# An expert layer on one core: two loads of x with other rows, and two copies behind each group of transposes

## The chip, the cores and the metric

The kernel runs on one core of a Trainium2 chip. Its engines work side by side and wait for each other through semaphores: TensorE (PE; PEld are its weight loads), VectorE (DVE), ScalarE (ACT), GpSimd (POOL) and SyncE (SP). Sixteen DMA engines move data between the memory of the chip (HBM, "dram" in the profile) and the core's own SBUF; transfers are issued here from SP's queue and from POOL's, and POOL's also turn float32 into bfloat16 on the way. TensorE writes into PSUM, from where DVE and ACT copy to SBUF. SBUF and PSUM have 128 partitions.

The metric is the device time of one execution in microseconds. Before the change it is 179.24 us, the median of three runs (179.19 to 179.28).

## The reference

Eight experts, each with its own 256 tokens of 512 numbers, go through two matrices with a ReLU between them:

```python
n_experts, capacity, hidden, expert_hidden = 8, 256, 512, 2048
# x  [8, 256, 512]   w1 [8, 512, 2048]   w2 [8, 2048, 512], all float32

def reference(x, w1, w2):
    h = np.matmul(x, w1)
    h = np.maximum(h, 0)
    return np.matmul(h, w2).astype(np.float32)
```

x is 4.2 MB, each of w1 and w2 is 33.6 MB, the output 4.2 MB.

## The kernel before

All matrix work is in bfloat16. The 2048 rows of x (experts one after the other, 512 numbers of 2 KB each) are laid over the partitions 16 at a time: partition p holds rows 16p to 16p+15, which are 32 KB of memory in one run (R is 16). The first six of them (HEAD) come through SP: a float32 load into a part of `out_sb` that is still free (L136, the first instruction of SP), which DVE then casts into `x_sb` (L215). The other ten come through POOL, which casts in the transfer (L154). `x_sb` is no buffer of its own; it lies in slot 2 of `w2_sb`.

TensorE needs x with the hidden dimension on the partitions, so it transposes it first (loop `transposes`). One turn of the loop takes every fourth column (turn ko, K1 = 4 turns). In a turn there are two groups of eight 128x128 transposes, one into each of two PSUM buffers `xt_ps[m]`; group m takes the rows r with r = 2·r2 + m of every partition, r2 = 0 to 7. Behind group 0 DVE copies `xt_ps[0]` to `xT`, behind group 1 ACT copies `xt_ps[1]` (both `copy_xt`, L206 to L210). The copy also puts the columns in order: PSUM has them by r2 and then by partition, `xT` by partition and then by r2, so that each expert's tokens lie together. TensorE takes `c_xt[0]` or `c_xt[1]` before it writes a buffer again, and both once more behind the loop (L331). Before the loop it waits for DVE's cast, for the identity matrix and for POOL's half of x (L324 to L326).

Then a loop over the experts. An expert takes `c_w1`, makes its hidden layer in four groups of 16 matmuls (`half`, twice), each of which ACT turns into `hT` with a ReLU (L240), takes `c_w2` and adds up two output tiles in 32 matmuls, which DVE copies to `out_sb` (L226; the very last one ACT, L246).

The weights come through POOL alone, in the order of the list `loads`: w1 and w2 for experts 0 and 1 together, the same for 2 and 3, w1 for 4 and 5, then w2 of 4, w2 of 5, and w1 and w2 of 6 and of 7, the last w2 in two halves. There are four slots for each matrix. Three kinds of wait stand in POOL's program in front of its transfers: w2 of experts 2 and 3 waits for all transposes, because its slot holds x (L172); each load into a used slot waits until the expert that used it is through; the stores wait for the outputs. SP waits for each load in turn (L143) and then tells TensorE through `c_w1` and `c_w2`. At the end SP stores the last expert's output (L146), POOL all the others (L194).

Lines to know: L136 and L154 load x; L172 is POOL's wait for the transposes; L191 issues the weights; L207 is the copy out of PSUM; L276 stands for every matmul and transpose, since all go through one helper.

Of the kernel before, what the change touches and what calls it, by code (L numbers as in the profile page):

```python
# [16 lines left out]
def kernel(  # L17
# [7 lines left out]
    nc = tc.nc  # L25
    P = 128
    E, C, H = x.shape
    F = w1.shape[2]
    MC = C // P
# [3 lines left out]
    R = E * C // P  # L33

    HEAD = 6
# [10 lines left out]

    x_v = x.rearrange("e (pp r) k -> (e pp) (r k)", r=R)
    w1_v = w1.rearrange("e (p ko) n -> p e (ko n)", ko=K1)  # L50
    w2_v = w2.rearrange("e (p h j) n -> p e h (j n)", h=2, j=JH)
    out_v = out.rearrange("e (p mo) k -> p e (mo k)", mo=MC)
# [4 lines left out]
    def allot(name, shape, dtype):  # L57
        nonlocal free
        places[name] = free
        t = nc.alloc_sbuf_tensor_at(name, shape, dtype, offset=free)  # L60
        free += math.prod(shape[1:]) * mybir.dt.size(dtype)
        return t
# [5 lines left out]
    xT = allot("xT", [P, K1, MC, E * P], BF16)  # L68
# [4 lines left out]
    x_sb = w2_sb[:, 2, :]  # L73
    X_AT = W2_AT + 2 * K2 * H * 2

    xt_ps = [nc.alloc_psum_tensor(f"xt_ps{i}", [P, R // MC, P], BF16) for i in range(MC)]
# [5 lines left out]
    def sem(name):  # L82
        s = nc.alloc_semaphore(name)
        sems.append(s)
        return s

    d_last, d_pool = sem("d_last"), sem("d_pool")
# [6 lines left out]
    d_head, d_half = sem("d_head"), sem("d_half")  # L94
# [38 lines left out]

    x_head = out_sb[:, :HEAD // MC].rearrange("p e m h -> p (e m h)")

    head = nc.sync.dma_start(x_head, x_v[:, :HEAD * H]).then_inc(d_head, 16)  # L136
    tc.info.no_tile_sem_insts.add(head.ins.name)
    tc.close()
    tc.compile()  # L139
# [11 lines left out]


    pool = nc.gpsimd
    pool.dma_start(x_sb[:, HEAD * H:], x_v[:, HEAD * H:]).then_inc(d_pool, 16)  # L154
    pool.memset(identity[:], 0.0).then_inc(s_event)  # L155
    pool.wait_ge(s_event, 1)

# [9 lines left out]
    for i, (w, es, h, n) in enumerate(loads):  # L167
# [17 lines left out]
        e, ne, at_slot = es[0], len(es), es[0] % NS  # L185
# [18 lines left out]


    def copy_xt(copy, ko, m):  # L206
        return copy(  # L207
            xT[:, ko, m].rearrange("k (ep r2) -> k ep r2", r2=R // MC),
            xt_ps[m][:].rearrange("k r2 ep -> k ep r2"),
        )  # L210


    dve = nc.vector
# [3 lines left out]
    for ko in range(K1):  # L217
        dve.wait_ge(*after_transposes(ko * MC + 1))
        copy_xt(dve.tensor_copy, ko, 0).then_inc(c_xt[0])
# [14 lines left out]
    for ko in range(K1):  # L234
        act.wait_ge(*after_transposes(ko * MC + 2))
        copy_xt(act.copy, ko, 1).then_inc(c_xt[1])
# [239 lines left out]
```

## Time and profile before

| | |
|---|---|
| median of three runs | 179.24 us |
| the profiled execution | 179.49 us, of which its span is 178.2 us |
| TensorE busy | 127.1 us (71% of the span) |
| DVE / ACT / POOL busy | 16.4 / 38.7 / 10.2 us |
| DMA: POOL's queue / SP's queue | 38.54 MB / 2.10 MB |
| read from HBM / written to it | 71.30 MB / 4.20 MB |
| mean granted TensorE clock | 0.943 |

The span runs from the first to the last instruction; the time of an execution has some more around it. A digit in a line of slices is the busy share of one fortieth of the span in tenths. A row of a group of instructions has the line, the engine, the operation, what it writes and reads, how often, then busy time and the mean of one in ns, then the idle time of the engine ahead of them and what ended it. A row in order of time begins with its start and its length in us. The sizes and rates of a transfer count what is written; where POOL's transfer casts, twice as much is read.

### The profile page before, as it was taken

To read this page: it belongs to the slowest core of one execution; us is meant where nothing else is said; L and a number is where in the kernel's file an instruction comes from. 1 tells how busy PE (TensorE), PEld (TensorE's weight loads), DVE (VectorE), ACT (ScalarE), POOL (GpSimd) and SP (SyncE) were. 2 spreads that over 40 slices of the span, in tenths; PEclk is the share of its full clock that TensorE was granted. 3 is DMA by queue.
4 is the path that set the end of the run, shared out by engine and by line. 5 is a ranking of instruction groups with operands and counts; after the bars stand their busy time and mean duration, and the time that the engine had idled before them with its cause. 6 is when DMAs were issued, how large, how long until landed. Compare 5 with 4: busy or idle time off the path is not lost. (4 is left out here: it accounts for less than half of the span.)

```text
span 178.2 us, 2076 instructions
## 1 busy us (share of the span) xinstructions
PE 127.1 (71%) x832; PEld 89.6 (50%) x832; DVE 16.4 (9%) x20; ACT 38.7 (22%) x38; POOL 10.2 (6%) x21
## 2 busy tenths in 40 slices
PE   0007620692039999994069999999999999949991
PEld 0006520592013695594024884794695695438740
DVE  0303420000000200110000200200200200020001
ACT  2002420053000053044000251152062044004401
POOL 4300010000000002001000100100010000001000
PEclk9999999999657999999759999999999999978999
DMA  5999999999999999998998999999999999999998
GB/s 199 299 212 232 232 195 221 232 195 221 232 210 206 232 217 199 232 224 191 232 228 188 235 228 195 224 232 195 221 232 195 221 232 210 206 204 223 298 418 328
DMA packets 3744, 40.63 MB, mean 228 GB/s; under 512 B 288, under 2 KB 288, under 8 KB 1312
## 3 DMA queue, kind: packets, MB, share of 16 engines
q0 software_dynamic: 3456, 38.54, 96.9%
q1 hardware_dynamic: 288, 2.10, 3.1%
HBM read 71.30 MB, written 4.20 MB: 424 GB/s over the span
## 5 line engine op out<-in xcount | busy, mean ns | idle before, releaser
L276 PE MATMUL o_ps<-w_sb,hT 128*128 x256 | 59.8, 394 | 19.5 <-PEq L99 19.5
L276 PE MATMUL h_ps<-xT,w_sb 128*128 x512 | 61.2, 282 | 11.8 <-PEq L99 11.8
L276 PEld LDWEIGHTS h_ps<-xT,w_sb 128*128 x512 | 57.8, 146 | 16.1 <-issue 12.5
L240 ACT ACTIVATE hT<-h_ps 128x1024 bf16<-128x1024 f32 x32 | 32.7, 1023 | 111.2 <-PE h_ps L276 111.2
L276 PEld LDWEIGHTS o_ps<-w_sb,hT 128*128 128x128 bf16 x256 | 25.3, 101 | 51.5 <-issue 24.5
L226 DVE COPY out_sb<-o_ps 128x512 f32<-128x512 f32 x15 | 9.7, 686 | 141.3 <-PE o_ps L276 141.3
L276 PE MATMUL xt_ps<-identity,w_sb 128*128 128x128 bf16 x64 | 7.6, 313 | 16.0 <-PEq L99 16.0
L276 PEld LDWEIGHTS xt_ps<-identity,w_sb 128*128 x64 | 6.5, 148 | 16.7 <-issue 16.7
L191 POOL DMA_DIRECT2D w_sb<-in_w_dram x12 | 7.4, 618 | 103.4 <-PE h_ps L276 57.1
L207 ACT COPY xT<-xt_ps 128x1024 bf16<-128x1024 bf16 x4 | 4.0, 1012 | 17.3 <-PE xt_ps L276 17.3
L207 DVE COPY xT<-xt_ps 128x1024 bf16<-128x1024 bf16 x4 | 4.9, 1224 | 10.1 <-PE xt_ps L276 10.1
L194 POOL DMA_DIRECT2D out_dram<-out_sb x1 | 1.0, 964 | 34.2 <-DMA out_dram<-out_sb 34.2
L215 DVE CAST w_sb<-out_sb 128x3072 bf16<-128x3072 f32 x1 | 1.8, 1760 | 7.2 <-DMA out_sb<-in_x_dram 7.2
L246 ACT COPY out_sb<-o_ps 128x512 f32<-128x512 f32 x1 | 0.6, 585 | 5.9 <-PE o_ps L276 5.9
L207 ACT ACT_TABLE_LOAD x1 | 1.3, 1283 | 2.0 <-PEq L139 2.0
L182 POOL DMA_DIRECT2D out_dram<-out_sb x1 | 0.5, 509 | 14.7 <-DVEq L229 14.7
L154 POOL DMA_DIRECT2D w_sb<-in_x_dram x1 | 0.7, 682 | 2.0 <-POOLq L139 2.0
L158 POOL TENSOR_SCALAR_AFFINE_SELECT identity<-identity 128x128 bf16<-128x128 bf16 x1 | 0.3, 282 | 0.2 <-POOL identity L155 0.2
L155 POOL MEMSET identity<- 128x128 bf16 x1 | 0.2, 223 | 0.0
L460 POOL MEMSET const-float32-0.0<- 128x1 f32 x1 | 0.1, 93 | 0.2 <-issue 0.2
L460 POOL MEMSET const-bfloat16-1.0<- 128x1 bf16 x1 | 0.1, 95 | 0.0
L460 POOL MEMSET const-uint8-127<- 128x1 uint8 x1 | 0.1, 95 | 0.0
(1 smaller groups left out, 0.1 us busy)
## 6 DMA issues: line engine op xcount, KB each, us to landing
w_sb<-in_w_dram POOLq DMA_DIRECT2D x5, 4096.0 KB, 47.2
w_sb<-in_w_dram POOLq DMA_DIRECT2D x5, 2048.0 KB, 51.8
out_dram<-out_sb POOLq DMA_DIRECT2D x1, 3584.0 KB, 12.8
w_sb<-in_w_dram POOLq DMA_DIRECT2D x2, 1024.0 KB, 44.3
out_sb<-in_x_dram SPq DMA_DIRECT2D x1, 1536.0 KB, 6.4
w_sb<-in_x_dram POOLq DMA_DIRECT2D x1, 1280.0 KB, 10.8
out_dram<-out_sb SPq DMA_DIRECT2D x1, 512.0 KB, 3.1
out_dram<-out_sb POOLq DMA_DIRECT2D x1, 1.0 KB, 34.7
```

The source lines that it names most:

```text
L154: pool.dma_start(x_sb[:, HEAD * H:], x_v[:, HEAD * H:]).then_inc(d_pool, 16)
L158: pool.affine_select(out=identity[:], in_=identity[:], compare_op=mybir.AluOpType.not_equal, fill=1.0, base=0, pattern=[[-1, P]], channel_ ...
L182: pool.dma_start(out_v[:16, 0, :16], out_sb[:16, 0, 0, :16]).then_inc(d_pool, 16)
L191: pool.dma_start(dst, src).then_inc(landed[i][0], 16)
L194: pool.dma_start(out_v[:, :E - 1, :], out_sb[:, :E - 1].rearrange("p e m h -> p e (m h)")).then_inc(d_pool, 16)
L207: return copy(xT[:, ko, m].rearrange("k (ep r2) -> k ep r2", r2=R // MC), xt_ps[m][:].rearrange("k r2 ep -> k ep r2"),)
L215: dve.tensor_copy(x_sb[:, :HEAD * H], x_head).then_inc(s_cast)
L226: cp = dve.tensor_copy(out_sb[:, e, m, :], o_ps[m][:])
L240: act.activation(hT[:, g * GJ:(g + 1) * GJ, :].rearrange("p a c -> p (a c)"), h_ps[g % UG][:], mybir.ActivationFunctionType.Relu,).then_in ...
L246: act.copy(out_sb[:, E - 1, 1, :], o_ps[1][:]).then_inc(v_last)
L276: return pe.add_instruction(inst)
L460: nc = _bacc.Bacc("TRN2", target_bir_lowering=False, num_devices=1)
```

## The change

x is divided between the two loads in another way. SP's load takes the first 768 rows of x, six after six to the partitions: partition p holds rows 6p to 6p+5. POOL's takes the other 1280 rows, ten after ten: partition p holds rows 768+10p to 768+10p+9. Each of the two sources is now one piece of memory without gaps; before, each load took 12 KB or 20 KB out of every 32 KB. The places in SBUF, the sizes and the queues stay as they are.

The transposes are the same instructions. But the first three results of a group (r2 = 0, 1, 2) now belong to the first 384 columns of `xT` of that m, the other five to the remaining 640, and each part has its own order. So `copy_xt` issues two copies, one of 3 x 128 and one of 5 x 128 columns, and the semaphore is incremented by the second alone.

```diff
-    x_v = x.rearrange("e (pp r) k -> (e pp) (r k)", r=R)
+
+    x_rows = x.rearrange("e t k -> (e t) k")
+    x_head_v = x_rows[:HEAD * P].rearrange("(p r) k -> p (r k)", r=HEAD)
+    x_rest_v = x_rows[HEAD * P:].rearrange("(p r) k -> p (r k)", r=R - HEAD)
...
-    head = nc.sync.dma_start(x_head, x_v[:, :HEAD * H]).then_inc(d_head, 16)
+    head = nc.sync.dma_start(x_head, x_head_v).then_inc(d_head, 16)
...
-    pool.dma_start(x_sb[:, HEAD * H:], x_v[:, HEAD * H:]).then_inc(d_pool, 16)
+    pool.dma_start(x_sb[:, HEAD * H:], x_rest_v).then_inc(d_pool, 16)
...
     def copy_xt(copy, ko, m):
-        return copy(
-            xT[:, ko, m].rearrange("k (ep r2) -> k ep r2", r2=R // MC),
-            xt_ps[m][:].rearrange("k r2 ep -> k ep r2"),
-        )
+
+        at = 0
+        for a, b in [(0, HEAD // MC), (HEAD // MC, R // MC)]:
+            inst = copy(
+                xT[:, ko, m, at:at + (b - a) * P].rearrange("k (ep r2) -> k ep r2", r2=b - a),
+                xt_ps[m][:, a:b].rearrange("k r2 ep -> k ep r2"),
+            )
+            at += (b - a) * P
+        return inst
```

## The prediction

> **What bounds the kernel now.** I read the page first for the shares, then the chain of waits, then stretches of the span, then the start in order of time.
>
> ```profile
> span 178.2 us, 2076 instructions
> PE 127.1 (71%) x832; PEld 89.6 (50%) x832; DVE 16.4 (9%) x20; ACT 38.7 (22%) x38; POOL 10.2 (6%) x21
> DMA  5999999999999999998998999999999999999998
> q0 software_dynamic: 3456, 38.54, 96.9%
> q1 hardware_dynamic: 288, 2.10, 3.1%
> ```
>
> The DMA engines are full in every slice but the first. No compute engine is. The chain that ended last begins only at 158.5 us:
>
> ```profile
> 158.53 0.04 issue
> 158.57 8.87 PE h_ps L276 x64
> 167.44 6.97 PE o_ps L276 x32
> 174.41 0.02 issue
> 174.43 0.58 ACT out_sb L246
> ```
> ```profile
> 158.57 8.87 PE L276 MATMUL h_ps<-xT,w_sb 128*128 x64 [2.62 <-PEq L99]
> ```
>
> The second fence is the same place in the order of time: TensorE stood still for 2.62 us before it, so the last expert's w1 had to land first. The end is therefore: the stream of loads up to that landing, then 15.9 us of TensorE work, then the last copy and store. Whatever makes the two loads of x at the head of the stream shorter or longer moves the end by as much; whatever happens on other engines under the stream costs nothing.
>
> The stages, as stretches of the span (columns: stretch, length, busy time and count of PE, PEld, DVE, ACT, POOL, granted clock, DMA share, GB/s as written):
>
> ```profile
> 1.70:3.50 1.80, 0.00 (x0) 0.00 (x0) 0.00 (x0) 1.28 (x1) 0.90 (x2) 1.00 0.94 266
> 3.50:6.00 2.50, 0.00 (x0) 0.00 (x0) 0.00 (x0) 0.00 (x0) 2.30 (x4) 1.00 1.01 428
> 7.00:12.00 5.00, 0.00 (x0) 0.00 (x0) 1.76 (x1) 0.00 (x0) 0.00 (x0) 1.00 1.01 213
> 13.20:32.50 19.30, 7.57 (x64) 6.53 (x64) 4.90 (x4) 4.05 (x4) 0.72 (x1) 1.00 1.02 217
> 24.60:32.70 8.10, 0.00 (x0) 0.00 (x0) 0.00 (x0) 0.00 (x0) 0.00 (x0) 1.00 0.95 202
> 129.40:139.00 9.60, 9.60 (x68) 6.87 (x67) 0.00 (x0) 3.83 (x4) 0.46 (x1) 1.00 1.02 218
> ```
>
> SyncE's load of x keeps float32, so its 428 GB/s are also what it reads. Pool's loads turn float32 into bfloat16, so they read twice what they write: 426 GB/s for x, 434 and 436 for weights.
>
> **The change part by part.**
>
> Transfers. Two x loads stay two x loads, on the same queues, issued at the same places, with the same bytes (1.573 MB read by SyncE's, 2.621 MB by Pool's) to the same columns. No instruction is passed on SP or POOL, no wait is added there. Only the addresses in memory differ: 12 KB out of every 32 KB becomes 12 KB after 12 KB, 20 KB out of every 32 becomes 20 after 20. Does a transfer that is one piece get cut differently? The two stretches of time 0:15 and 158:178 of the DMA view say no:
>
> ```profile
> q1 hardware_dynamic: 144, 1.57, 28.4%
> ```
> ```profile
> q1 hardware_dynamic: 144, 0.52, 6.4%
> ```
>
> The first is x with its gaps, the second the last expert's store, which is one piece in memory without a gap (its rows p·2 and p·2+1 for p after p). Both are 144 packets: cut by partition, not by runs of memory. And is a source without gaps faster? Row 13.20:32.50 is the pair load of experts 0 and 1 (in each partition two runs of 32 KB that lie 4 MB apart): 217. Row 129.40:139.00 is, by its place in the queue (19.3 us for each 4 MB from 13.2 on), expert 6's w1 alone, without any gap: 218. That is half a per cent, the rounding of the view. By these rows the layout is worth nothing to a stream under way.
>
> What is there to gain at most: at the weights' 434, Pool's 2.621 MB take 6.04 us and not 6.15 (0.11); the steady part of SyncE's load, 2.5 us at 428, gains 0.03. The ramp 1.70:3.50 moved 0.479 MB, which at 434 take 1.10 us: 0.70 us are lost there. All three together are 0.84 us. To lose: the nearest row of a slow load is that same ramp; a ramp as costly again is +0.70. I take 0.05 us of gain: the rows nearest to the changed transfers are the steady ones, and the ramp is that of the first transfer after idle engines, which any layout has. Ends: -0.84 and +0.70.
>
> One rule bears on it. In the Trainium skill, DMA: Bandwidth & Descriptors, section Latency and other measured facts, a large power-of-two distance from one partition's row to the next costs rate (207 GB/s at 512 KiB where full is 214), and contiguous tiles are the remedy. The distance here is 32 KB, which that table does not reach; 207/214 taken on all of x (4.194 MB at 428 GB/s are 9.8 us) would be an estimate of 0.33 us of gain. The trace has 426 against 434, 1.9%, so it neither needs nor excludes the rule.
>
> Copies. Eight copies of xT become sixteen, of 384 and 640 columns. The rows:
>
> ```profile
> L226 DVE COPY out_sb<-o_ps 128x512 f32<-128x512 f32 x15 | 9.7, 686 | 141.3 <-PE o_ps L276 141.3
> L207 ACT COPY xT<-xt_ps 128x1024 bf16<-128x1024 bf16 x4 | 4.0, 1012 | 17.3 <-PE xt_ps L276 17.3
> L207 DVE COPY xT<-xt_ps 128x1024 bf16<-128x1024 bf16 x4 | 4.9, 1224 | 10.1 <-PE xt_ps L276 10.1
> L246 ACT COPY out_sb<-o_ps 128x512 f32<-128x512 f32 x1 | 0.6, 585 | 5.9 <-PE o_ps L276 5.9
> ```
>
> DVE: 512 columns more cost 1224-686 = 538 ns, so one instruction has 686-538 = 148 ns that do not go with columns. ACT: 1012-585 = 427, and 158 ns. Each group so becomes 0.15 us (DVE) or 0.16 us (ACT) longer, 4 x 0.148 = 0.59 us of DVE time in all and 0.63 of ACT. Where do they lie?
>
> ```profile
> 7.21 1.76 DVE L215 CAST w_sb<-out_sb 128x3072 bf16<-128x3072 f32 x1 [7.21 <-DMA out_sb<-in_x_dram]
> 13.76 1.89 PE L276 MATMUL xt_ps<-identity,w_sb 128*128 128x128 bf16 x16 [13.76 <-PEq L99]
> 14.83 1.23 DVE L207 COPY xT<-xt_ps 128x1024 bf16<-128x1024 bf16 x1 [5.86 <-PE xt_ps L276]
> 17.46 1.22 DVE L207 COPY xT<-xt_ps 128x1024 bf16<-128x1024 bf16 x1 [1.40 <-PE xt_ps L276]
> 23.57 1.01 ACT L207 COPY xT<-xt_ps 128x1024 bf16<-128x1024 bf16 x1 [1.61 <-PE xt_ps L276]
> 23.83 0.72 POOL L191 DMA_DIRECT2D w_sb<-in_w_dram  x1 [17.66 <-PE xt_ps L276]
> 32.74 3.49 PE L276 MATMUL h_ps<-xT,w_sb 128*128 x18 [9.21 <-PEq L99]
> ```
>
> One turn of the loop is 2.63 us (14.83 to 17.46): DVE's copy, then TensorE's eight transposes into the freed bank, then the next copy. TensorE is the one queued behind DVE. With 0.15 more a turn is 2.78; three turns put the last ACT copy 0.44 later and its own second instruction makes it 0.16 longer, so it ends at 24.58+0.60 = 25.2. TensorE starts on experts at 32.74, when w1 of experts 0 and 1 has landed; the row 24.60:32.70 shows all compute engines idle. Cover: 8.1 us before, 7.5 after. Short inner runs (3 and 5 elements where there were 8) have no row; if a pair of copies cost twice one copy, four turns grow by 4.9 us and end at 29.5, still covered. I take 0.60 us, on the path: 0. Without that cover the whole 0.60 would be paid.
>
> The other who waits for the transposes is POOL, which issues w2 of experts 2 and 3 at 23.83 (L172's wait), and behind it all later loads. It would be 24.3. Its bytes come fourth in a queue whose three loads ahead take 19.3 us each from 13.2, so not before 71 us: 47 us of cover. The wait for SyncE's half (DVE's cast) ends at 7.21, long before Pool's half, for which TensorE waits until 13.7.
>
> Sum: transfers -0.05, copies 0, POOL 0. Profiled execution 179.49 us (178.2 of span and 1.29 around it) becomes 179.44; the median of the runs lies 0.25 under the profiled one, so 179.24-0.05 = 179.2. A measurement of this kernel tells about 0.2% (0.36 us) from no change; my forecast is no change by that bound.
>
> **The rivals.**
>
> Ramp shortened (faster). Before, the 16 engines' first pieces lie whole multiples of 32 KB apart; if that is why the ramp moves 266 and not 428, pieces 12 KB apart spread better. For it: the ramp's 0.70 us is the one place in the stream far under rate. Against it: row 13.20:32.50 reads runs of 32 KB just as regularly spaced, at full rate. Between 0.36 and 0.84 us: about 0.5, 178.7.
>
> Ramp lengthened (slower). The end hangs on the last of 16 engines, since a load counts as landed when all shares are in. The new address order may give one engine a slower first piece, and it carries that lateness through to 158.5, because no engine ever idles. For it: the stream has no gap in which to catch up (shares of 8 and 9 throughout). Against: nothing in the steady rows differs by layout. It decides from 0.36 us of the last engine; at the bound +0.70: 179.9, likely 179.7.
>
> Half clock moved. In the last stage TensorE ran at half its clock:
>
> ```profile
> 158.50:161.80 3.30, 3.23 (x16) 2.54 (x17) 0.00 (x0) 0.00 (x0) 0.00 (x0) 0.50 1.05 221
> 60.91 7.28 PE L276 MATMUL h_ps<-xT,w_sb 128*128 x64
> 52.09 8.98 PE L276 MATMUL o_ps<-w_sb,hT 128*128 x32 [10.71 <-PEq L99]
> 167.33 7.07 PE L276 MATMUL o_ps<-w_sb,hT 128*128 x32
> ```
>
> The 64 matmuls took 8.87 us and at full clock 7.28: 1.59 us on the path. If the start of that stage shifts against the clock's stretches, they could be saved (177.6); or, if a half-clock stretch falls on o_ps too, 8.98-7.07 = 1.91 us are added (181.1). Against both: the idle time ahead (2.62 us) is set by loads that all shift together, and three runs lie within 0.09 us. TensorE: Matmul & The Clock Gate in the Trainium skill (Part 1) has the monitor's window free-running at 3413 ns; then no change of this kind sets its phase, and the 3.30 us at 0.50 here fit that length.
>
> Copies show. The 8.1 us are used up when a turn grows by over 2.0 us, so a pair of copies takes over 3.2 us where one takes 1.22. At 3.5 us a pair the end moves by 4 x 2.28 - 8.1 = 1.0: 180.2. No row is near that.
>
> That the change does nothing at all for memory is my own forecast, not a rival.
>
> **How the numbers follow.** No change within 0.2%: 0.46 (179.2, own range 178.9 to 179.6). Ramp shortened: 0.27. Ramp lengthened: 0.19. Half clock, either way: 0.06, half of it faster. Copies show: 0.02, slower. Faster 0.30, same 0.46, slower 0.24. The time is that of the likeliest; the range, 178.5 to 179.8, goes over nearly all of the ramp's two bounds and leaves out the clock, the copies and the far ends.
>
> **What would show it.** Sixteen L207 copies of about 0.5 and 0.8 us, last end near 25.2, TensorE's first h_ps still near 32.7, POOL's fourth weight load near 24.3: right on the copies. SyncE's load landing (start of DVE's cast) at 7.21 and TensorE's first transpose at 13.76, within 0.1 us: right on the transfers; each tenth by which the transposes start earlier or later should stand again at 158.5 and at the end. Wrong if the first transpose moves by over 0.3 us, if the GB/s of x's stretches leave 428 and 213, or if the 64 matmuls of the last stage do not take 8.9 us.

## The result

The changed kernel takes 179.66 us (median of eight runs, 179.43 to 180.04) where the kernel before takes 179.22 (eight runs beside them). The ratio is 1.0026, with a 95% interval of 1.0017 to 1.0035: slower by about 0.4 us. The profiled execution took 179.73 us, with a span of 178.4 us; before it was 179.49 and 178.2. So one execution shows half of the difference of the medians (0.24 of 0.44).

The page of the changed kernel, first the shares, then the DMA slices and queues:

```profile
span 178.4 us, 2076 instructions
PE 127.2 (71%) x824; PEld 89.9 (50%) x832; DVE 16.6 (9%) x24; ACT 38.9 (22%) x42; POOL 10.2 (6%) x21
DMA  5999999999999999999999999999999999999997
q0 software_dynamic: 3456, 38.54, 96.8%
q1 hardware_dynamic: 288, 2.10, 3.2%
```

The transfers have as many packets and bytes as before, and the engines are as full. The start in order of time, changed kernel:

```profile
0.74 0.38 SPq L139 DMA_DIRECT2D out_sb<-in_x_dram  x1
2.41 0.68 POOL L157 DMA_DIRECT2D w_sb<-in_x_dram  x1 [1.96 <-POOLq L142]
...
7.43 1.76 DVE L223 CAST w_sb<-out_sb 128x3072 bf16<-128x3072 f32 x1 [7.43 <-DMA out_sb<-in_x_dram]
...
13.98 1.89 PE L284 MATMUL xt_ps<-identity,w_sb 128*128 128x128 bf16 x16 [13.98 <-PEq L102]
15.05 1.29 DVE L213 COPY xT<-xt_ps 128x384 bf16<-128x384 bf16 x2 [5.86 <-PE xt_ps L284]
...
23.98 1.07 ACT L213 COPY xT<-xt_ps 128x384 bf16<-128x384 bf16 x2 [1.62 <-PE xt_ps L284]
24.24 0.72 POOL L194 DMA_DIRECT2D w_sb<-in_w_dram  x1 [18.08 <-PE xt_ps L284]
...
32.95 3.40 PE L284 MATMUL h_ps<-xT,w_sb 128*128 x15 [9.01 <-PEq L102]
...
158.79 8.85 PE L284 MATMUL h_ps<-xT,w_sb 128*128 x64 [2.62 <-PEq L102]
```

Before, the first row was

```profile
0.74 0.38 SPq L136 DMA_DIRECT2D out_sb<-in_x_dram  x1
```

Read the first column against the rows of before: SyncE's load is issued at the same 0.74 and its data are all there at 7.43 (7.21 before); the first transpose starts at 13.98 (13.76), the first h_ps at 32.95 (32.74), the last expert at 158.79 (158.57), the span ends at 178.4 (178.2). The lateness is there when SyncE's load has landed, about 0.22 us, and it is neither made up nor added to in the following 170 us. The copies sit between and change nothing in it.

Two stretches of the changed kernel's span, columns as in the prediction's table:

```profile
1.70:3.50 1.80, 0.00 (x0) 0.00 (x0) 0.00 (x0) 1.28 (x1) 0.90 (x2) 1.00 0.95 218
3.50:6.00 2.50, 0.00 (x0) 0.00 (x0) 0.00 (x0) 0.00 (x0) 2.30 (x4) 1.00 1.03 426
```

The ramp moves 218 GB/s where it moved 266; the steady part is the same (426 and 428). 1.8 us at 48 GB/s less are 0.086 MB, which at 434 GB/s are 0.2 us. The trace also records each of the 128 pieces of SyncE's load, one for each partition. Those that start from 3 us on take 0.46 us (median) in both kernels, although in the changed one they lie as near to each other as the first ones. Those that start before 3 us, 24 and 22 of them on 16 engines, take 0.83 us on average before and 1.03 us after the change. So the loss lies in the first one or two pieces of each engine.

The landing of a load is counted in 16 steps, here called its shares. The first share of SyncE's load lands earlier than before (6.21 us, 6.40 before) and the last later (7.41, 7.19): the engines get through it less evenly. POOL's load of x is next in the stream, and its last share lands at 13.43 instead of 13.20. That sets the end: in both traces the span ends 164.98 us after it. Of the 17 traces of this study in which SyncE's load goes first, 15 end 164.96 to 164.98 us after that landing (the other two 165.09 and 165.56).

### The profile page after: what moved, and what is told of

Its sections match the earlier page's. It is cut to its first block, busy times and chain, and to the rows that moved or that the text cites. A ratio compares the mean times of both kernels' runs of the same rounds, so it can differ in the third digit from the quotient of the medians.

```text
span 178.4 us, 2076 instructions
## 1 busy us (share of the span) xinstructions
PE 127.2 (71%) x824; PEld 89.9 (50%) x832; DVE 16.6 (9%) x24; ACT 38.9 (22%) x42; POOL 10.2 (6%) x21
## 5 line engine op out<-in xcount | busy, mean ns | idle before, releaser
L213 ACT COPY xT<-xt_ps 128x384 bf16<-128x384 bf16 (+1 forms) x8 | 4.3, 588 | 17.5 <-PE xt_ps L284 17.5
L213 DVE COPY xT<-xt_ps 128x384 bf16<-128x384 bf16 (+1 forms) x8 | 5.2, 686 | 10.1 <-PE xt_ps L284 10.1
```

Source lines behind the costliest of these rows:

```text
L213: inst = copy(xT[:, ko, m, at:at + (b - a) * P].rearrange("k (ep r2) -> k ep r2", r2=b - a), xt_ps[m][:, a:b].rearrange("k r2 ep -> k ep r2"),
```

## The experiments

Each median stands beside the kernel before on the same chip (179.16 to 179.26 us in the six groups). The ratio is not that of the two medians; the two differ by up to 0.1%. Kernels that read some rows of x twice and others not at all say so in their expectation.

**Which part costs it.** Four kernels, each with one part of the change or two.

Copies alone:

```diff
     def copy_xt(copy, ko, m):
+        whole = xT[:, ko, m].rearrange("k (ep r2) -> k ep r2", r2=R // MC)
+        for a, b in [(0, HEAD // MC), (HEAD // MC, R // MC)]:
+            inst = copy(whole[:, :, a:b], xt_ps[m][:, a:b].rearrange("k r2 ep -> k ep r2"))
+        return inst
```

> The rows of x are divided between the two loads as before; only the copies out of PSUM are two per group (of 384 and 640 columns, into every column of xT that belongs to them). Theory A (the loss comes from the first pieces of SyncE's load, which in the changed kernel spread the 16 engines further apart): no difference, within 0.15 us of the kernel before; last xT copy near 25.0 us, first h_ps as before near 32.7. Rival B (the copies cost it, through POOL's later issue or the clock): the whole +0.44 us here.

179.17 us, ratio 0.9991 (0.9982 to 1.0000): nothing lost. Its transposes ended later within the loop and its span did not:

```profile
13.44 1.89 PE L276 MATMUL xt_ps<-identity,w_sb 128*128 128x128 bf16 x16 [13.44 <-PEq L99]
14.51 1.40 DVE L209 COPY xT<-xt_ps 128x384 bf16<-128x384 bf16 x2 [5.88 <-PE xt_ps L276]
...
24.05 0.72 POOL L191 DMA_DIRECT2D w_sb<-in_w_dram  x1 [17.87 <-PE xt_ps L276]
32.40 1.90 PE L276 MATMUL h_ps<-xT,w_sb 128*128 x8 [8.65 <-PEq L99]
```

TensorE stood still for 8.65 us ahead of the first h_ps all the same. These copies write runs of three and five columns with gaps between them, which the changed kernel's do not, and a pair takes longer than there (1.40 us on DVE, 1.29 in the changed kernel); even so they cost nothing at the end. Rival B falls.

Both loads with one copy per group (the changed kernel with the old `copy_xt`):

```diff
     def copy_xt(copy, ko, m):
+        return copy(
+            xT[:, ko, m].rearrange("k (ep r2) -> k ep r2", r2=R // MC),
+            xt_ps[m][:].rearrange("k r2 ep -> k ep r2"),
+        )
```

> Both loads of x without gaps as in the changed kernel, but one copy per group as before, so the tokens come out in another order within the output (the reordering is left out). Theory A: +0.3 to +0.6 us as the changed kernel, first transpose near 14.0 instead of 13.76. Rival B: no difference.

179.62 us, ratio 1.0016 (1.0007 to 1.0025), 0.39 us by the medians: the loads carry the loss.

SyncE's load alone, and POOL's alone:

```diff
-    head = nc.sync.dma_start(x_head, x_v[:, :HEAD * H]).then_inc(d_head, 16)
+    head = nc.sync.dma_start(x_head, x_head_v).then_inc(d_head, 16)
```

> Only SyncE's load takes 768 rows in one piece; POOL's takes 20 KB out of every 32 KB as before (so some rows come twice and others not at all: a time only). Theory A: +0.3 to +0.6 us, the whole loss, with the last of SyncE's shares landing 0.2 us or more later than 7.2. Rival C (POOL's load loses it, by its new places): within 0.15 us of before.

```diff
-    pool.dma_start(x_sb[:, HEAD * H:], x_v[:, HEAD * H:]).then_inc(d_pool, 16)
+    pool.dma_start(x_sb[:, HEAD * H:], x_rest_v).then_inc(d_pool, 16)
```

> Only POOL's load takes its 1280 rows in one piece; SyncE's takes 12 KB out of every 32 KB as before (some rows twice, others not at all: a time only). Theory A: within 0.15 us of before. Rival C: +0.3 to +0.6 us, and the stretch of POOL's x load below 213 GB/s as written.

SyncE's: 179.70 us, 1.0023 (1.0014 to 1.0031). POOL's: 179.27 us, 1.0003 (0.9993 to 1.0014). All of the loss is in SyncE's load; the same step taken on POOL's costs nothing that can be measured. In order of time, SyncE's load alone, then POOL's alone:

```profile
9.02 1.76 DVE L217 CAST w_sb<-out_sb 128x3072 bf16<-128x3072 f32 x1 [9.02 <-DMA out_sb<-in_x_dram]
...
14.09 1.89 PE L278 MATMUL xt_ps<-identity,w_sb 128*128 128x128 bf16 x16 [14.09 <-PEq L101]
```
```profile
6.83 1.76 DVE L217 CAST w_sb<-out_sb 128x3072 bf16<-128x3072 f32 x1 [6.83 <-DMA out_sb<-in_x_dram]
...
13.40 1.89 PE L278 MATMUL xt_ps<-identity,w_sb 128*128 128x128 bf16 x16 [13.40 <-PEq L101]
```

With SyncE's load alone changed, its last share lands 1.8 us later than before, and the first transpose starts only 0.33 us later. So the landing of SyncE's load by itself is no measure of the loss; that of POOL's behind it, for which the transposes wait, is. The other kernel loads SyncE's rows as the kernel before does. Its profiled execution took 179.13 us, and that of the copies alone 179.17; the last share of POOL's load lands at 12.85 and 12.88 us there. The profiled execution of the kernel before (179.49) was a late one, with 13.20, which is why a comparison with it shows only half of the loss. Against those two the changed kernel's 13.43 is 0.55 to 0.58 us later.

**Missing gaps, or the distance of the pieces?** The 12 KB pieces of SyncE's load were laid at other distances, with gaps; q is the distance in rows of 2 KB.

```diff
+    x_head_v = x_rows[:q * P].rearrange("(p r) k -> p (r k)", r=q)[:, :HEAD * H]
-    head = nc.sync.dma_start(x_head, x_v[:, :HEAD * H]).then_inc(d_head, 16)
+    head = nc.sync.dma_start(x_head, x_head_v).then_inc(d_head, 16)
```

> As the kernel before, but SyncE's 12 KB pieces begin every 14 KB (gaps of 2 KB) and not every 32 KB; POOL's load as before, so some rows come twice and others not at all: a time only. Theory G (the missing gaps cost it): as before, within 0.15 us. Theory S (pieces that lie closer together let the 16 engines start less evenly, the more the closer): +0.35 us or more, nearly the +0.47 of the 12 KB distance. Theory D (certain distances collide, others not): either.

> The same with a piece every 16 KB (gaps of 4 KB). Theory G: within 0.15 us of before. Theory S: +0.3 us. Theory D: a power of two like the 32 KB of the kernel before, so as before, or far worse.

> The same with a piece every 20 KB. Theory G: within 0.15 us of before. Theory S: +0.2 to +0.3 us. Theory D: an odd multiple of 4 KB, like 12 KB, so +0.3 us or more.

> The same with a piece every 24 KB. Theory G: within 0.15 us of before. Theory S: +0.1 to +0.2 us. Theory D: between those of 12 and 32 KB.

> SyncE's 12 KB pieces begin every 28 KB; POOL's as before (a time only). Theory S (the closer the pieces the later the last engine): between 24 KB (+0.26) and 32 KB (0), so +0.1 us. Theory D (certain distances collide): an odd multiple of 4 KB like 20 KB, so +0.3 us or more.

| a piece every | median us | against before | ratio (95%) |
|---|---|---|---|
| 12 KB (SyncE's load alone, above) | 179.70 | +0.47 | 1.0023 (1.0014 to 1.0031) |
| 14 KB | 179.61 | +0.45 | 1.0018 (1.0008 to 1.0028) |
| 16 KB | 179.94 | +0.78 | 1.0033 (1.0019 to 1.0046) |
| 20 KB | 179.75 | +0.59 | 1.0023 (1.0009 to 1.0037) |
| 24 KB | 179.42 | +0.26 | 1.0013 (1.0003 to 1.0023) |
| 28 KB | 179.48 | +0.25 | 1.0019 (1.0009 to 1.0029) |
| 32 KB (the kernel before) | 179.16 to 179.26 | 0 | 1 |

Theory G falls: 14 KB has gaps and loses as much. Every distance that was tried under 32 KB is slower, by its medians 0.45 us or more up to 20 KB and about 0.25 at 24 and 28. That is the direction of theory S, but its sizes are missed at 16 and 20 KB (0.78 and 0.59 where it had 0.3 and 0.2 to 0.3), and the intervals overlap, so the course between is not settled. D is not excluded: it allowed 16 KB to be far worse and had 0.3 us or more at 20 KB, but also at 28 KB.

At 16 KB the trace shows a second loss. The pieces that start from 3 us on take 0.51 us on average (0.46 in the kernel before), and the first share of SyncE's load lands at 6.91 us (6.40): there all engines are late, and not only some. Nor does the rate of the ramp rank these kernels; at 20 KB it is 266 GB/s, as before the change.

Is it the place in x? The last 768 rows in one piece:

```diff
+    x_head_v = x_rows[-HEAD * P:].rearrange("(p r) k -> p (r k)", r=HEAD)
```

> SyncE's load takes 768 rows in one piece again, but the last 768 of x and not the first; POOL's as before (some rows twice, others not at all: a time only). If the small distance between pieces is what costs: +0.3 to +0.6 us, as with the first 768. If it is something about the place at the head of x: within 0.15 us of before.

179.59 us, 1.0026 (1.0013 to 1.0039). It is not the place.

**When does the distance cost?** First, a small load ahead of SyncE's, in the kernel before and in the changed one:

```diff
+    first = nc.sync.dma_start(out_sb[:, E - 1, 1, :16], w1_v[:, E - 1, :16]).then_inc(d_head, 16)
     head = nc.sync.dma_start(x_head, x_v[:, :HEAD * H]).then_inc(d_head, 16)
...
-    dve.wait_ge(d_head, 16)
+    dve.wait_ge(d_head, 32)
```

> As the kernel before, with a load of 64 bytes per partition on SyncE's queue ahead of x (from w1, into a place that is written over later), so that x is no longer the first transfer of the engines; DVE waits for both. It pays SyncE's issue of about 0.4 us where nothing hides it: +0.2 to +0.5 us, or less if the engines start more evenly for it.

> As the changed kernel, with the same small load ahead. To be compared with the run of the kernel before with that small load. Theory 1 (the distance costs only where idle engines start a transfer in step for the first time): the two are equal within 0.15 us. Theory 2 (the distance costs whenever the 16 engines begin a transfer together, first or not): this one is 0.3 to 0.6 us slower than the other.

179.74 us (1.0031, 1.0019 to 1.0043) and 180.14 us (1.0052, 1.0039 to 1.0066). The difference, 0.40 us, is the whole loss of the change: that some bytes have already been moved does not help. Theory 1 falls. In both traces the small load's pieces are through by 2.2 us and the first pieces of x start from 2.2 us on, so the engines begin on x afresh.

Second, SyncE's load cut into two transfers of three rows each, far pieces (every 32 KB) or near ones (one behind the other):

```diff
-    head = nc.sync.dma_start(x_head, x_v[:, :HEAD * H]).then_inc(d_head, 16)
+    head = nc.sync.dma_start(x_head[:, 0 * H:3 * H], x_v[:, :3 * H]).then_inc(d_head, 16)
+    head = nc.sync.dma_start(x_head[:, 3 * H:6 * H], x_rows[3 * P:6 * P].rearrange("(p r) k -> p (r k)", r=3)).then_inc(d_head, 16)
```

(far first, near second; the others accordingly, and DVE waits for 32.)

> SyncE's load of x in two transfers of three rows each (6 KB pieces), issued one behind the other, both with a piece every 32 KB: the control of the next two. Two issues instead of one: 0 to +0.3 us against the kernel before; below it only if smaller first pieces let the engines start more evenly.

> The same two transfers; the first with a piece every 32 KB, the second with its 6 KB pieces one behind the other (some rows twice, others not at all: a time only). Theory 3 (only the moment counts at which all 16 engines begin on idle queues): as the control, within 0.15 us. Theory 4 (near pieces cost wherever they are read): 0.2 to 0.5 us slower than the control.

> The same two transfers the other way round: the first with its pieces one behind the other, the second with a piece every 32 KB (a time only, too). Theory 3: the whole loss, 0.3 to 0.6 us slower than the control. Theory 4: 0.2 to 0.5 us slower, as the other order.

Far and far: 179.33 us, 1.0001 (0.9990 to 1.0011). Far and near: 179.55, 1.0013 (1.0005 to 1.0022). Near and far: 179.52, 1.0016 (1.0007 to 1.0024). The medians of both orders are about 0.2 us above the control's, half of the whole loss, with intervals that overlap the control's. The traces do not put it down to the near pieces. In far and near the first transfer, whose pieces lie far apart, already lands late (last share 5.56 us, 5.31 in the control), and the near pieces behind it, from 4.2 us on, take 0.235 us on average where the far ones of the control take 0.246. In near and far POOL's load lands earlier than in the control (13.10, 13.18), and that execution loses its time later in the stream. Each of the two is the slowest execution of its kernel. So neither theory is shown: theory 4 has no support in the pieces' times, and where the 0.2 us of the medians arise stays open.

Third, the roles exchanged: SyncE issues its load only when POOL's has landed, so that POOL's is the one that finds idle engines.

```diff
-    head = nc.sync.dma_start(x_head, x_v[:, :HEAD * H]).then_inc(d_head, 16)
...
     sp = nc.sync
+    sp.wait_ge(d_pool, 16)
+    sp.dma_start(x_head, x_v[:, :HEAD * H]).then_inc(d_head, 16)
```

> As the kernel before, but SyncE issues its load of x only when POOL's has landed, so POOL's is the first on idle engines and SyncE's runs beside the weights. The control of the next two. The bytes are the same; the idle start moves to POOL's later issue (2.4 us where SyncE's was 0.7): +1 to +2.5 us.

> The same with SyncE's 768 rows in one piece (some rows twice, others not at all: a time only). Theory 5 (near pieces cost only in the load that starts the idle engines): as the control, within 0.15 us. Theory 6 (near pieces cost on SyncE's queue at any time): 0.3 to 0.6 us slower than the control.

> The same control with POOL's 1280 rows in one piece, now the first load on idle engines (a time only, too). Theory 5: slower than the control, by 0.3 to 0.6 us as for a piece every 20 KB in SyncE's load. Theory 6: within 0.15 us of the control.

Control 180.97 us (1.0091, 1.0077 to 1.0105). With SyncE's pieces near: 180.91 (1.0086, 1.0073 to 1.0100), so nothing lost. With POOL's pieces near: 181.76 (1.0134, 1.0119 to 1.0150), 0.79 us more than the control, and more than the 0.3 to 0.6 that were expected. It is not the queue: near pieces cost in the load that starts idle engines, whichever queue it is on, and cost nothing beside a stream that runs. Theory 5 holds. In order of time, the start of the control, and then of the kernel with POOL's pieces near:

```profile
1.89 0.68 POOL L154 DMA_DIRECT2D w_sb<-in_x_dram  x1 [1.45 <-POOLq L137]
11.06 0.38 SPq L141 DMA_DIRECT2D out_sb<-in_x_dram  x1
```
```profile
1.89 0.68 POOL L156 DMA_DIRECT2D w_sb<-in_x_dram  x1 [1.45 <-POOLq L139]
11.80 0.38 SPq L143 DMA_DIRECT2D out_sb<-in_x_dram  x1
```

SyncE's issue marks the landing of POOL's load: 11.06 and 11.80. The 0.74 us between them are nearly all of the 0.79 at the end, and they are those of a single share: the other 15 have landed by 10.87 us in both.

No kernel of this study is clearly faster than the kernel before.

## Why the prediction was wrong

What it got right. The copies: it expected about 0.5 and 0.8 us and no effect. By form, the changed kernel has

```profile
L213 DVE COPY xT<-xt_ps 128x640 bf16<-128x640 bf16 x4 | 3.3, 814 | 0.0
L213 ACT COPY xT<-xt_ps 128x640 bf16<-128x640 bf16 x4 | 2.8, 697 | 0.0
L213 DVE COPY xT<-xt_ps 128x384 bf16<-128x384 bf16 x4 | 2.2, 558 | 10.1 <-PE xt_ps L284 10.1
L213 ACT COPY xT<-xt_ps 128x384 bf16<-128x384 bf16 x4 | 1.9, 480 | 17.5 <-PE xt_ps L284 17.5
```

From its 148 ns and 538 ns for 512 columns, DVE's two come to 551 and 820 ns; 558 and 814 were measured, so reading short inner runs cost nothing of its own here. (In the kernel with the copies alone, which writes such runs with gaps between them, 384 columns took DVE 735 ns and 640 took 801.) The two copies overlap a little: a pair takes 1.29 us and not 1.37, and a turn 2.69 us (13.98 to 16.67 in the trace) and not 2.78. POOL's fourth weight load at 24.24 and the last copy's end at 25.05 are where it put them (24.3 and 25.2), but by luck: the copies delayed POOL by 0.19 us after the first transpose and not by 0.44, and the late loads added 0.22. The steady rates (426 and 428, Pool's load alone +0.04 us by its medians) did not depend on the layout either. The prediction's signs for the transfers, a first transpose within 0.1 us for right and over 0.3 us off for wrong, left the 0.22 us of this trace undecided.

The step that failed: "the ramp is that of the first transfer after idle engines, which any layout has". The layout sets how costly that ramp is: the pieces that start before 3 us took 1.03 us on average instead of 0.83. Of the terms of the sum it is the one entered as 0.05 us of gain, between ends of -0.84 and +0.70; it was a loss of 0.44 by the medians, 0.39 with both loads alone and 0.47 with SyncE's alone. The rows it was taken from, 217 GB/s for a load with jumps of 4 MB and 218 for one without, are true, but they are rows of a stream that runs, and the transfer that was changed was the one that starts it. The rival "ramp lengthened" had the mechanism, the place and the size (from 0.36 us to 0.70, carried by the last engine to 158.5), with a chance of 0.19 and against it only those same steady rows. It had one engine late where the trace has eight of 16, and no reason why the new order should be the slow one. The rival "ramp shortened" had the direction upside down: pieces 12 KB apart do not spread better than pieces 32 KB apart, they start less evenly. The rule of the Trainium skill on row distances (DMA: Bandwidth & Descriptors, Latency and other measured facts), taken down to 32 KB, pointed the wrong way: it holds large powers of two to be costly and contiguous tiles to be a remedy, and here 32 KB was the best of seven distances and the contiguous layout slower. Its figures begin at 512 KiB and are for copies between tensors in HBM, so no run here tests the rule itself.

A second step was wrong without moving the number: "then 15.9 us of TensorE work". The last stage is bound by the DMA engines as well. The order of time at the end of the kernel in which POOL's load alone is changed and comes second:

```profile
158.20 7.32 PE L278 MATMUL h_ps<-xT,w_sb 128*128 x64 [2.09 <-PEq L101]
...
172.51 0.59 ACT L248 COPY out_sb<-o_ps 128x512 f32<-128x512 f32 x1 [5.93 <-PE o_ps L278]
173.12 0.35 SPq L148 DMA_DIRECT2D out_dram<-out_sb  x1
```

and its two large stores in the DMA view:

```profile
out_dram<-out_sb POOLq DMA_DIRECT2D x1, 3584.0 KB, 12.8
out_dram<-out_sb SPq DMA_DIRECT2D x1, 512.0 KB, 4.7
```

The same of the kernel before, in order of time and in the DMA view:

```profile
175.04 0.35 SPq L146 DMA_DIRECT2D out_dram<-out_sb  x1
```
```profile
out_dram<-out_sb POOLq DMA_DIRECT2D x1, 3584.0 KB, 12.8
...
out_dram<-out_sb SPq DMA_DIRECT2D x1, 512.0 KB, 3.1
```

In that execution the clock was not halved (granted clock 1.00 from 158.2 to 165.0 us), the 64 matmuls took 7.32 us instead of 8.87, and the last store was issued at 173.12 instead of 175.04. But it landed 4.7 us later instead of 3.1, at 177.8, behind POOL's store of 3584 KB: in both traces 1.23 us after the last share of that store. The span was 177.8 instead of 178.2. TensorE won 1.9 us and the end 0.4, which is what the loads were earlier (first transpose at 13.40 instead of 13.76). So the price of the half clock, 1.59 us, is hidden, and the faster half of the rival built on it was worth nothing; its slower half came up in no trace. The 15 traces that end 164.96 to 164.98 us after the landing of POOL's load say the same: in eight of them the 64 matmuls take 8.9 us, in seven 7.3. The chain of waits had not shown it, since it names TensorE and ACT and then stops at the last instruction, not at the last landing.

The cover of the transposes was understated in the same way. In the three kernels with SyncE's load behind POOL's the first h_ps starts at 43 to 44 us instead of 32.74. Their spans end 168.69 us after the last share of POOL's load, where the others have 164.98. The 3.71 us between are SyncE's 1.573 MB, which now come behind that landing, at 424 GB/s; nothing is left for TensorE. So 10 us more at its first expert are covered too.

## What to carry to other kernels

In a kernel bound by its DMA stream, cost a changed load by where it stands in the stream: rates of a running stream say nothing of the load that finds all engines idle, and here the lateness that arose there went to the end unchanged. A layout without gaps is no gain in itself; here the largest distance between the pieces of the first load, 32 KB, was the best (none larger was tried). And when a chain of waits ends on a compute engine, compare the last issue and the last landing before costing anything on that engine.

## What was not expected of the hardware

Near pieces in the first load cost 0.25 to 0.78 us at distances of 12 to 28 KB against 32 KB, in SyncE's first load (0.47 at 12 KB) and in POOL's where it comes first (0.79 at 20 KB), and nothing in either when it comes second (-0.06 and +0.04 us). In the traces of the changed kernel and of SyncE's load alone the loss lies in the first pieces of each engine. In all four traces with the first 768 rows in one piece, eight of the 16 shares of SyncE's load land as a group behind the other eight (in the changed kernel from 6.87 us on, the others by 6.65); with the last 768 rows they do not, and the loss is much the same. Why near pieces slow the start was not found out: no view shows where in memory a transfer waits, and with POOL's load first a single share carries the loss.
